# Routing two experts first, spreading small work over experts 1 and 2, and transposing act between two chunks of the down projection

## The chip, the cores and the metric

The kernel runs on one core of one Trainium2 chip. The metric is the device time of one execution in microseconds (us), as the median of several runs. Its engines are TensorE (PE, with its weight loads shown apart as PEld), VectorE (DVE), ScalarE (ACT), GpSimd (POOL, which here issues the indirect DMAs and some others) and SyncE (SP, which issues the weight loads).

## The reference, cut to what matters

The model is one layer: a sparse attention and a state-space branch are mixed, and then a mixture of 32 experts works on 512 tokens of width 1024. Only the experts are touched by the change.

```python
logits = (hf @ w_router + b_router)              # 512 tokens, 32 experts
top_val, top_idx = lax.top_k(logits, 4)          # four experts for each token
gates = softmax(top_val)
# for each expert, in blocks of 128 tokens:
gu = xb @ w_gu[e] + b_gu[e]                      # 1024 -> 2048
g, u = minimum(gu[:, :1024], 7), clip(gu[:, 1024:], -7, 7)
act = (u + 1.0) * (g * sigmoid(1.702 * g))
out = act @ w_dn[e] + b_dn[e]                    # 1024 -> 1024
x = x + g_f * sum over a token's experts of gate * out
```

## The kernel before

After the two branches, the kernel computes the router's logits, marks each token's four experts and ranks the tokens of each expert (`rankm`). Then it walks through the 32 experts, one block of 128 tokens each. A loop behind it (`tc.For_i`) takes experts with over 128 tokens; how often it turns is worked out as `nbt` from the counts `cnt`, through `more` and `cum`.

**Weights.** Each expert has twelve chunks of 1 MB (128 x 2048), eight for `w_gu` and four for `w_dn`. SP loads them in order into ten buffers. `msplit` makes two fp32r parts of each: ACT writes the high part (L1318), DVE the low part (L1319). PE multiplies three times per tile: high by high, high by low and low by high (L1468 to L1470), so that a chunk is 12 matmuls. Four split chunks stand ready; `refill` splits the next one when PE has used one up. The split tiles come from two pools in turn, `stm` (whi, wlo) and `M` (mhi, mlo).

**One expert.** An expert is two halves (f = 0, 1). Each half has a `group` for the gate columns (two chunks, with a bias matmul), a group for the up columns, four transposes of the next expert's tokens `xg` (L1270), and a group of the down projection of the expert before (`prev`). Behind that down group stand four transposes of this expert's `act`; ACT and DVE copy them as `ah` and `al`, which the next expert's down groups read. `gated` and `upped` (L1281, L1285, L1286) make `act` from the groups' sums, and L1533 scales the down result into `y`. From expert 1 on PE, DVE and ACT follow the order of the program text (`tc.manual_schedule`). POOL and SP do not: a planner orders their instructions. Expert 0 and all before it are ordered by the planner on every engine, except what `keep_in_program_order` pins.

**Routing.** For each expert a `one_hot` (128 x 512, L1004, DVE) is made, PE multiplies it with `aux` ("picks", into the PSUM tile `mi`), and a few small DVE operations turn the sums into `gi` (the rows to gather), `si` (the rows to add to) and `gate`. Expert 0 is routed alone, experts 1 to 3 together (`route(groups[0])`), and then four experts at a time in `routed`: its steps are queued and taken one by one by `hot_step`, which is called six times in an expert, behind each of its six groups. With four experts there are five steps that build a one-hot and pick the one before, and a sixth, `end`, that makes `gi`.

```python
groups = {0: [1, 2, 3]}
groups.update({e: list(range(e + 3, min(e + 7, NE))) for e in range(1, NE - 3, 4)})
```

The gates themselves are worked out late (`shares`, `gates_of`), behind expert 0's first gate group. The one-hots of pool `M` have two buffers.

**Gather and put.** `gather(e)` (POOL, L1376) brings the 128 token rows of expert e, 512 KB, from DRAM into `xg`, which has two buffers. In the text, expert e asks for the rows of expert e + 2 at its end, and expert e + 1 transposes them, the first half behind its first up group. `put` (POOL, L1289) adds `y` to the rows of the output in DRAM. Both use the same DMA queue.

```python
if f and e + 2 < NE:
    xg = gather(e + 2)
```

**Other work at the start.** `shared_biases` brings the down biases into a `y` tile, clears its last rows (L1396), and splits them; `shared_down(t)` (L1417, L1418) adds gates times biases to the output for each of four blocks of tokens. All four stand behind expert 0's second half, and the chain from `more` to `nbt` (L1452 to L1460) behind them.

Of the kernel before, what the change touches and what calls it, by code (L numbers as in the profile page):

```python
# [11 lines left out]
F32 = mybir.dt.float32  # L12
F32R = mybir.dt.float32r
BF = mybir.dt.bfloat16
I32 = mybir.dt.int32
# [7 lines left out]
P = 128  # L23
# [4 lines left out]
NE = 32  # L28
# [105 lines left out]
def program(tc, A, dbg=None, upto=99):  # L134
# [5 lines left out]
    with ctx:  # L140
# [66 lines left out]
        with ExitStack() as c1:  # L207
# [241 lines left out]
            for t in range(NT):  # L449
                T.transpose(p[:, t * P:(t + 1) * P], kin[:, t, :], ident)  # L450
            S.activation(kiT, p, AF.Identity, bias=gain[:, 3:4], scale=gain[:, 2:3])
            wi8 = con.tile([P, NT, 8], F32, name="wi8")
            V.tensor_scalar(wi8, s88[:, :, 64:72], 8 ** -0.5, None, op0=OP.mult)
            say("kiT", kiT, [P, L])

# [134 lines left out]
                                 scale=qk_gain[:, which:which + 1])  # L590


            cw = con.tile([P, 60], F32, name="cw")
            V.tensor_scalar(cw, convc, 0.5, None, op0=OP.mult)
            xdt = big("C", [P, NT, D])
            yD = quarters()
# [627 lines left out]
        def block_parts(M, mp, nbuf):  # L1224
# [61 lines left out]
                V.scalar_tensor_tensor(act, act, SILU7, u, op0=OP.min, op1=OP.mult)  # L1286

            def put(y, si, out=out):
                G.indirect_dma_start(out=out, out_offset=bass.IndirectOffsetOnAxis(ap=si, axis=0), in_=y,  # L1289
                                     in_offset=None, compute_op=OP.add)  # L1290

            def all_picked(p, i, hot, aux_of):
# [11 lines left out]
        with ExitStack() as c2:  # L1304
# [22 lines left out]
            def refill(pin=False):  # L1327
                if ahead:
                    parted.append(msplit(ahead.pop(0), pin))
                mload()  # L1330
# [24 lines left out]
                        T.matmul(p, x[1][:, kk, :], hi[:, ws], start=False, stop=(kk == KD - 1))  # L1355
                return p

            groups = {0: [1, 2, 3]}
            groups.update({e: list(range(e + 3, min(e + 7, NE))) for e in range(1, NE - 3, 4)})
            info = {}  # L1360

            def route(es):
# [27 lines left out]
            def shared_biases():  # L1390

                b = mt([P, KD, P], F32R, name="ah").rearrange("p k c -> p (k c)")
                raw = sized("y")
                for r in range(0, 96, 32):
                    G.dma_start(raw[r:r + 32, :], A["b_dn"])
                V.memset(raw[96:P, :], 0.0)  # L1396
                S.activation(b, raw, AF.Copy)
                V.tensor_tensor(b[32:64, :], raw[32:64, :], b[32:64, :].bitcast(F32), op=OP.subtract)
                gg = mt([P, 2, NT, P], F32R, name="al")
                gc, gT = gg[:, 0].rearrange("p t (a e) -> p t a e", e=NE), gg[:, 1]  # L1400
                V.memset(gc[:, :, 3, :].bitcast(F32), 0.0)
                for a in range(2):
                    V.tensor_copy(gc[:, :, a, :], gates)
                V.tensor_tensor(gc[:, :, 2, :], gates, gc[:, :, 0, :].bitcast(F32), op=OP.subtract)
                p = mp.tile([P, NT, P], F32, name="tr", tag="tr", bufs=2)
                for t in range(NT):
                    T.transpose(p[:, t, :], gg[:, 0, t, :].bitcast(F32), ident)
                S.activation(gT, p, AF.Copy)
                return gT, b
# [24 lines left out]
            for f in range(2):  # L1434
                fs = slice(f * 512, (f + 1) * 512)
                u = mt([P, 512], name="u", bufs=1)
                gated(act[:, fs], three(xT, bias["b_gu"], 0, f * 512, "gu", 3))
                if f == 0:
                    shares()
                    gates_of([0])  # L1440
                    gates_of(groups[0])
                upped(u, three(xT, bias["b_gu"], 0, FE + f * 512, "gu", 3), act[:, fs])
                if f == 0:
                    shared = shared_biases()
                    xT_next = transposed(xg, "x")
                    xg = gather(2)
                else:
                    for t in range(NT):
                        shared_down(t, *shared)
                aT = transposed(act, "a", b=f, into=aT, scale=1.0 / ALPHA)  # L1450
            few = mt([P, NE], name="few", bufs=1)
            tc.keep_in_program_order(V.tensor_scalar(more, cnt, 128.5, None, op0=OP.is_gt))  # L1452
            for lim in (256.5, 384.5):
                V.tensor_scalar(few, cnt, lim, None, op0=OP.is_gt)
                V.tensor_tensor(more, more, few, op=OP.add)
            V.tensor_copy(cum, more)
            for d in (1, 2, 4, 8, 16):
                V.tensor_copy(few, cum)
                V.tensor_tensor(cum[:, d:], few[:, d:], few[:, 0:NE - d], op=OP.add)
            V.tensor_copy(nbt, cum[:, NE - 1:NE])  # L1460

# [5 lines left out]
                    T.matmul(p, x[0][:, kk, :], lo[:, ws], start=False, stop=False)  # L1469
                    T.matmul(p, x[1][:, kk, :], hi[:, ws], start=False, stop=(kk == KD - 1))  # L1470

            def group(x, e, c0, take):
                if c0 is None:
                    p = mp.tile([P, 512], F32, name="dn", tag="dn", bufs=2)
                else:
# [4 lines left out]
                for i in range(2):  # L1480
                    chunk(p, x, i, c0 is None)
                    if i:
                        take(p)
                    refill()

            routing = []

            def hot_step():

                if routing:  # L1490
                    routing.pop(0)()

            def routed(es):
                p = mp.tile([P, 512], F32, name="mi", tag="mi", bufs=1)[:, 0:6 * len(es)].rearrange("p (e c) -> p e c", c=6)
                hots = {}

                def step(i):
                    if i:
                        all_picked(p, i - 1, hots.pop(i - 1), lambda t: aux[:, t, es[i - 1], :])
                    if i < len(es):  # L1500
                        hots[i] = one_hot(M, es[i])

                def end():
                    gi, si, gate = all_of(p, len(es))
                    for i, e in enumerate(es):
                        info[e] = gi[:, i:i + 1], si[:, i:i + 1], gate[:, i:i + 1]

                return [lambda i=i: step(i) for i in range(len(es) + 1)] + [end]

            with tc.manual_schedule(engines={mybir.EngineType.PE, mybir.EngineType.DVE, mybir.EngineType.Activation}):  # L1510
                for e in range(1, NE + 1):
                    prev, xT, aT = aT, xT_next, None
                    if e < NE:
                        act = sized("act")
                        xT_next = None
                    y = sized("y")
                    if e in groups:
                        routing += routed(groups[e])
                    if e == NE:
                        halves_ = M.tile([P, 2], I32, name="halves")  # L1520
                        for f in range(2):
                            V.tensor_scalar(halves_[:, f:f + 1], info[e - 1][1], 2.0, float(f), op0=OP.mult, op1=OP.add)
                    for f in range(2):
                        fs = slice(f * 512, (f + 1) * 512)
                        if e < NE:
# [4 lines left out]
                            if e + 1 < NE:  # L1530
                                xT_next = transposed(xg, "x", b=f, into=xT_next)
                            hot_step()
                        group(prev, e - 1, None, lambda p: V.scalar_tensor_tensor(  # L1533
                            y[:, fs], p, info[e - 1][2], gf[:, fs], op0=OP.mult, op1=OP.mult))
                        if e < NE:
                            aT = transposed(act, "a", b=f, into=aT, scale=1.0 / ALPHA)
                            hot_step()
                        else:
                            put(y[:, fs], halves_[:, f:f + 1], out.rearrange("r (h c) -> (r h) c", h=2))
                        if f and e + 2 < NE:  # L1540
                            xg = gather(e + 2)
                    if e < NE:
                        put(y, info[e - 1][1])


        with ExitStack() as c3:
# [108 lines left out]
```

## Time and profile before

| | |
|---|---|
| median of three runs | 1827.83 us (1823.12 to 1829.53) |
| the profiled execution's own time | 1832.19 us |
| its span, first to last instruction | 1830.4 us |
| PE busy | 1761.2 us, 96% of the span |
| DVE busy | 1541.3 us, 84% |
| ACT busy | 1074.2 us, 59% |
| weight loads and other hardware-queue DMA | 469.70 MB |
| mean granted TensorE clock | 0.973 |

Busy is the time in which an engine worked on an instruction; DMA issues, waits and branches don't count. A busy PE is not one at its peak, because the ends of its matmuls are modelled. The clock is the share of full speed that PE was granted. Idle time of an engine that isn't the bottleneck costs nothing.

### The profile page before, as it was taken

To read this page: it belongs to the slowest core of one execution; us is meant where nothing else is said; L and a number is where in the kernel's file an instruction comes from. 1 tells how busy PE (TensorE), PEld (TensorE's weight loads), DVE (VectorE), ACT (ScalarE), POOL (GpSimd) and SP (SyncE) were. 2 spreads that over 40 slices of the span, in tenths; PEclk is the share of its full clock that TensorE was granted. 3 is DMA by queue.
4 is the path that set the end of the run, shared out by engine and by line. 5 is a ranking of instruction groups with operands and counts; after the bars stand their busy time and mean duration, and the time that the engine had idled before them with its cause. 6 is when DMAs were issued, how large, how long until landed. Compare 5 with 4: busy or idle time off the path is not lost. (4 is left out here: it accounts for less than half of the span.)

```text
span 1830.4 us, 22578 instructions
## 1 busy us (share of the span) xinstructions
PE 1761.2 (96%) x8540; PEld 1396.5 (76%) x8540; DVE 1541.3 (84%) x1877; ACT 1074.2 (59%) x1059; POOL 195.3 (11%) x114
## 2 busy tenths in 40 slices
PE   6999999999999679999999999999999999999997
PEld 3866877776678567888888888888888888888885
DVE  6486678865676779999999999999999999999995
ACT  3443333444323356776777777777777777777773
POOL 0000000000000111111111211111111111111101
PEclk9988999998799889999999999999999999999998
DMA  8242334432475489999999999999999999999991
GB/s 318 80 143 75 115 141 167 152 129 79 179 264 210 172 275 335 397 376 370 379 381 367 381 377 379 370 377 378 368 375 382 367 384 388 341 399 379 372 361 40
DMA packets 86455, 527.24 MB, mean 288 GB/s; under 512 B 10912, under 2 KB 11072, under 8 KB 32072
## 3 DMA queue, kind: packets, MB, share of 16 engines
q1 hardware_dynamic: 70552, 469.70, 66.5%
q0 software_dynamic: 15552, 55.97, 11.1%
q8 instruction: 68, 1.11, 0.2%
q14 instruction: 43, 0.35, 0.1%
q10 hardware_dynamic: 240, 0.10, 0.0%
HBM read 497.91 MB, written 30.45 MB: 289 GB/s over the span
## 5 line engine op out<-in xcount | busy, mean ns | idle before, releaser
L1319 DVE TENSOR_TENSOR wlo<-raw,whi 128x2048 fp32r<-128x2048 f32 x154 | 352.2, 2288 | 31.8 <-ACT whi L1318 31.8
L1319 DVE TENSOR_TENSOR mlo<-raw,mhi 128x2048 fp32r<-128x2048 f32 (+1 forms) x160 | 352.5, 2207 | 24.6 <-ACT mhi L1318 22.1
L1318 ACT ACTIVATE whi<-raw 128x2048 fp32r<-128x2048 f32 x154 | 295.4, 1918 | 115.3 <-PE gu L1470 66.8
L1318 ACT ACTIVATE mhi<-raw 128x2048 fp32r<-128x2048 f32 (+1 forms) x160 | 296.0, 1854 | 108.5 <-PE gu L1470 61.8
L1468 PE MATMUL gu<-whi,xh 128*128 128x512 f32 x496 | 196.4, 396 | 0.0
L1470 PE MATMUL gu<-whi,xl 128*128 128x512 f32 x496 | 196.4, 396 | 0.0
L1469 PE MATMUL gu<-wlo,xh 128*128 128x512 f32 x496 | 196.2, 396 | 0.0
L1470 PE MATMUL gu<-mhi,xl 128*128 128x512 f32 x496 | 193.6, 390 | 0.0
L1469 PE MATMUL gu<-mlo,xh 128*128 128x512 f32 x496 | 193.3, 390 | 0.0
L1468 PE MATMUL gu<-mhi,xh 128*128 128x512 f32 x496 | 193.3, 390 | 0.0
L1289 POOL DMA_INDIRECT out_dram<-y,si x31 | 104.3, 3364 | 465.5 <-DVE y L1533 465.5
L393 PE MATMUL mm<-B,whi 128*128 128x512 f32 x352 | 141.0, 400 | 0.0
L392 PE MATMUL mm<-bA,whi 128*128 128x512 f32 x320 | 131.3, 411 | 2.0 <-DVE brow L661 1.0
L394 PE MATMUL mm<-bA,wlo 128*128 128x512 f32 x320 | 128.4, 402 | 0.8 <-DVE wlo L185 0.8
L1376 POOL DMA_INDIRECT xg<-h2d,gi x32 | 62.2, 1945 | 543.5 <-PE tr L1270 500.3
L184 ACT ACTIVATE whi<-raw 128x2048 fp32r<-128x2048 f32 x34 | 65.0, 1914 | 85.9 <-PE mm L393 72.3
L1469 PEld LDWEIGHTS gu<-wlo,xh 128*128 128x128 f32 x496 | 93.3, 188 | 22.5
L1470 PEld LDWEIGHTS gu<-whi,xl 128*128 128x128 f32 x496 | 93.2, 188 | 22.5
L1468 PEld LDWEIGHTS gu<-whi,xh 128*128 128x128 f32 x496 | 93.5, 188 | 20.9 <-ACT xh L1271 0.2
L1469 PEld LDWEIGHTS gu<-mlo,xh 128*128 128x128 f32 x496 | 93.1, 188 | 20.2
L1470 PEld LDWEIGHTS gu<-mhi,xl 128*128 128x128 f32 x496 | 93.1, 188 | 19.7
L1468 PEld LDWEIGHTS gu<-mhi,xh 128*128 128x128 f32 x496 | 93.3, 188 | 18.6
(471 smaller groups left out, 3703.7 us busy)
## 6 DMA issues: line engine op xcount, KB each, us to landing
raw<-in_w_gu_dram SPq DMA_DIRECT2D x204, 1024.0 KB
raw<-in_w_dn_dram SPq DMA_DIRECT2D x104, 1024.0 KB
B<-in_w_gu_dram SPq DMA_DIRECT2D x52, 1024.0 KB
B<-in_w_dn_dram SPq DMA_DIRECT2D x24, 1024.0 KB
raw<-in_w_in_dram SPq DMA_DIRECT2D x23, 1024.0 KB
rawp<-in_w_ada_dram POOLq DMA_DIRECT2D x30, 512.0 KB, 4.1
bE<-in_w_ada_dram SPq DMA_DIRECT2D x4, 1024.0 KB
bC<-in_x_dram SPq DMA_DIRECT2D x8, 512.0 KB
```

Of the source, the lines that this page charges most:

```text
L184: S.activation(hi[:, 0:n], raw[:, 0:n], AF.Copy)
L392: T.matmul(p, wh, xT[0][:, k, :], start=(k == 0), stop=False)
L393: T.matmul(p, wh, xT[1][:, k, :], start=False, stop=False)
L394: T.matmul(p, wl, xT[0][:, k, :], start=False, stop=(k == nk - 1))
L1289: G.indirect_dma_start(out=out, out_offset=bass.IndirectOffsetOnAxis(ap=si, axis=0), in_=y, in_offset=None, compute_op=OP.add)
L1318: S.activation(hi[:, cs], raw[:, cs], AF.Copy)
L1319: i = V.tensor_tensor(lo[:, cs], raw[:, cs], hi[:, cs].bitcast(F32), op=OP.subtract)
L1376: G.indirect_dma_start(out=xg, out_offset=None, in_=h2d, in_offset=bass.IndirectOffsetOnAxis(ap=info[e][0], axis=0))
L1468: T.matmul(p, x[0][:, kk, :], hi[:, ws], start=(start and kk == 0), stop=False)
L1469: T.matmul(p, x[0][:, kk, :], lo[:, ws], start=False, stop=False)
L1470: T.matmul(p, x[1][:, kk, :], hi[:, ws], start=False, stop=(kk == KD - 1))
```

## The change

Eight edits stand together. `wi8` and `cw` move from the pool that lives to the end (`con`) to the one of the first part (`W`). `put` returns its instruction. The first routed set is experts 1 and 2; experts 3 to 5 are routed within expert 1, and from expert 4 on the sets of four begin at e + 2 in place of e + 3. The clearing of the bias rows is pinned to its place in the text. Two of the four `shared_down` move into the first two `hot_step` of expert 1, and the `nbt` chain, cut into ten steps, into those of experts 2 and 3; `y` is taken behind them. In `routed` a pick follows its one-hot by two steps, and `end` shares the step of the last pick. The transposes of `act` move between the two chunks of the down group (`mid`). The puts of the last two down results go out in halves, and the very last one is tied to the second half of the result before and not to the first half of its own.

```diff
-            wi8 = con.tile([P, NT, 8], F32, name="wi8")
+            wi8 = W.tile([P, NT, 8], F32, name="wi8")
...
-            cw = con.tile([P, 60], F32, name="cw")
+            cw = W.tile([P, 60], F32, name="cw")
...
-                G.indirect_dma_start(out=out, out_offset=bass.IndirectOffsetOnAxis(ap=si, axis=0), in_=y,
+                return G.indirect_dma_start(out=out, out_offset=bass.IndirectOffsetOnAxis(ap=si, axis=0), in_=y,
...
-            groups = {0: [1, 2, 3]}
-            groups.update({e: list(range(e + 3, min(e + 7, NE))) for e in range(1, NE - 3, 4)})
+            groups = {0: [1, 2], 1: [3, 4, 5]}
+            groups.update({e: list(range(e + 2, min(e + 6, NE))) for e in range(4, NE - 2, 4)})
...
-                V.memset(raw[96:P, :], 0.0)
+                tc.keep_in_program_order(V.memset(raw[96:P, :], 0.0))
...
-                    for t in range(NT):
+                    for t in range(2):
                         shared_down(t, *shared)
...
-            tc.keep_in_program_order(V.tensor_scalar(more, cnt, 128.5, None, op0=OP.is_gt))
...
+            def blocks_step(i):
+
+                if i == 0:
+                    V.tensor_scalar(more, cnt, 128.5, None, op0=OP.is_gt)
+                elif i < 3:
+                    V.tensor_scalar(few, cnt, 128.0 * i + 128.5, None, op0=OP.is_gt)
+                    V.tensor_tensor(more, more, few, op=OP.add)
+                elif i == 3:
+                    V.tensor_copy(cum, more)
+                elif i < 9:
+                    d = 1 << (i - 4)
+                    V.tensor_copy(few, cum)
+                    V.tensor_tensor(cum[:, d:], few[:, d:], few[:, 0:NE - d], op=OP.add)
+                else:
+                    V.tensor_copy(nbt, cum[:, NE - 1:NE])
...
-            def group(x, e, c0, take):
+            def group(x, e, c0, take, mid=None):
...
                     refill()
-
-            routing = []
+                    if mid and not i:
+                        mid()
+
+            routing, extra, added = [], [], []
...
-                if routing:
-                    routing.pop(0)()
+                for todo in (routing, extra):
+                    if todo:
+                        todo.pop(0)()
...
-                    if i:
-                        all_picked(p, i - 1, hots.pop(i - 1), lambda t: aux[:, t, es[i - 1], :])
+                    if i > 1:
+                        all_picked(p, i - 2, hots.pop(i - 2), lambda t: aux[:, t, es[i - 2], :])
                     if i < len(es):
                         hots[i] = one_hot(M, es[i])
+                    elif i > len(es):
+                        end()
...
-                return [lambda i=i: step(i) for i in range(len(es) + 1)] + [end]
-
+                return [lambda i=i: step(i) for i in range(len(es) + 2)]
+
+            box = [aT]
...
-                    y = sized("y")
+                    y = None
                     if e in groups:
                         routing += routed(groups[e])
-                    if e == NE:
-                        halves_ = M.tile([P, 2], I32, name="halves")
+                    if e == 1:
+                        extra += [lambda t=t: shared_down(t, *shared) for t in (2, 3)]
+                    if e == 2:
+                        extra += [lambda i=i: blocks_step(i) for i in range(10)]
+                    split_put = e >= NE - 1
+                    if split_put:
+                        halves_ = mt([P, 2], I32, name="halves")
...
+                        if f == 0:
+                            y = sized("y")
+                        if e < NE:
+                            def mid():
+                                box[0] = transposed(act, "a", b=f, into=box[0], scale=1.0 / ALPHA)
                         group(prev, e - 1, None, lambda p: V.scalar_tensor_tensor(
-                            y[:, fs], p, info[e - 1][2], gf[:, fs], op0=OP.mult, op1=OP.mult))
-                        if e < NE:
-                            aT = transposed(act, "a", b=f, into=aT, scale=1.0 / ALPHA)
-                            hot_step()
-                        else:
-                            put(y[:, fs], halves_[:, f:f + 1], out.rearrange("r (h c) -> (r h) c", h=2))
+                            y[:, fs], p, info[e - 1][2], gf[:, fs], op0=OP.mult, op1=OP.mult), mid if e < NE else None)
+                        hot_step()
+                        if split_put:
+                            added.append(put(y[:, fs], halves_[:, f:f + 1], out.rearrange("r (h c) -> (r h) c", h=2)).ins)
                         if f and e + 2 < NE:
                             xg = gather(e + 2)
-                    if e < NE:
+                    if not split_put:
                         put(y, info[e - 1][1])
+
+
+                tc.declare_no_dep(added[3], added[2], reason="disjoint halves of the rows")
+                tc.add_manual_dep(added[3], added[1].name, mybir.DependencyInfo(
+                    mybir.DependencyClass.Sync, mybir.DependencyReason.DATA), reason="rows of the expert before")
```

## Rows read from the trace of the kernel before

**Rows 1.** Windows (us from the start): length, busy time (instructions) of each engine, clock, DMA.
```profile
663.47:694.23 30.76, 21.65 (x96) 17.21 (x95) 23.49 (x38) 12.93 (x12) 9.42 (x7) 0.83 0.90 261
...
1055.69:1073.70 18.01, 18.01 (x86) 14.66 (x84) 16.71 (x12) 12.98 (x10) 0.00 (x0) 1.00 1.02 398
...
1127.92:1147.02 19.10, 18.91 (x99) 14.99 (x97) 18.73 (x15) 12.95 (x10) 0.00 (x0) 1.00 0.97 376
```

**Rows 2.** Waits from 740 to 1790 us: us in total, times, longest.
```profile
ACT whi L1318 <- PE gu L1470: 78.2, 87, 1.2
...
PE mi L1294 <- DVE hot L1004: 1.3, 6, 0.2
```

**Rows 3.** Timeline of 655 to 680 us, DVE, POOL and PE.
```profile
659.84 0.69 DVE L1004 TENSOR_TENSOR hot<-cst,ranks 128x512 bf16<-128x512 f32 x1
...
663.63 3.00 POOL L1376 DMA_INDIRECT xg<-h2d,gi  x1 [33.09 <-DVE gate L1257]
...
672.33 1.97 PE L1270 MATMUL tr<-cst,xg 128*128 128x128 f32 x8 [8.57 <-DMA xg<-h2d,gi]
```

**Rows 4.** Windows behind two idle stretches of PE, columns as in rows 1.
```profile
672.30:678.00 5.70, 5.67 (x21) 4.66 (x22) 3.29 (x6) 1.79 (x3) 1.77 (x2) 0.53 0.76 292
1810.90:1814.00 3.10, 3.10 (x9) 2.38 (x9) 0.23 (x1) 0.00 (x0) 0.00 (x0) 0.50 0.96 160
```

**Rows 5.** Timeline of the last 25 us, PE, POOL and DVE.
```profile
1809.90 0.51 PE L1470 MATMUL dn<-whi,al 128*128 128x512 f32 x1 [1.83 <-DVE al L1276]
...
1815.74 1.54 POOL L1289 DMA_INDIRECT out_dram<-y,halves  x1 [5.08 <-DMA out_dram<-y,si]
...
1819.71 0.75 DVE L1533 SCALAR_TENSOR_TENSOR y<-dn,gate,gf 128x512 f32<-128x512 f32 x1 [5.18 <-PE dn L1470]
...
1821.34 1.54 POOL L1289 DMA_INDIRECT out_dram<-y,halves  x1 [4.07 <-DVE y L1533]
```

**Rows 6.** Timeline of 623 to 637 us, DVE and POOL.
```profile
624.88 0.91 DVE L1396 MEMSET y<- 32x1024 f32 x1 [0.27 <-issue]
...
627.09 2.38 POOL L1376 DMA_INDIRECT xg<-h2d,gi  x1 [6.43 <-DVE gi L1246]
```

**Rows 7.** Groups of DVE's instructions, 663.47 to 694.23 us: busy, mean ns, idle before.
```profile
L1418 DVE TENSOR_TENSOR y<-dn,gf 128x512 f32<-128x512 f32 x8 | 5.3, 684 | 1.6 <-DMA out_dram<-y 1.4 <-PE dn L1417 0.2
...
L1459 DVE TENSOR_TENSOR cum<-few 128x31 f32<-128x31 f32 (+3 forms) x4 | 0.7, 179 | 0.0
```

**Rows 8.** Timeline of one half of an expert without routing, DVE and PE.
```profile
1765.28 0.69 DVE L1286 SCALAR_TENSOR_TENSOR act<-act,u 128x512 f32<-128x512 f32 x1
...
1766.24 0.39 PE L1468 MATMUL dn<-mhi,ah 128*128 128x512 f32 x1
```

**Rows 9.** Timeline around the end of expert 5, which routes, PE, DVE and POOL.
```profile
861.93 0.60 PE L1270 MATMUL tr<-cst,act 128*128 128x128 f32 x4
...
863.58 0.74 DVE L1533 SCALAR_TENSOR_TENSOR y<-dn,gate,gf 128x512 f32<-128x512 f32 x1
...
864.61 3.34 POOL L1289 DMA_INDIRECT out_dram<-y,si  x1 [33.75 <-DVE y L1533]
...
867.45 0.17 DVE L1246 CAST gi<-q 128x4 int32<-128x4 f32 x1
...
868.41 3.07 POOL L1376 DMA_INDIRECT xg<-h2d,gi  x1 [0.46 <-PE gu L1470]
...
873.90 0.60 PE L1270 MATMUL tr<-cst,xg 128*128 128x128 f32 x4
```

**Rows 10.** Gathers, us from issue to landing: one right behind a put; all 32.
```profile
xg<-h2d,gi POOLq DMA_INDIRECT x1, 10.8
...
DMA to landing us min/median/max: 4.2/9.5/13.9
```

**Rows 11.** Costliest groups of the page: busy, mean ns, idle before.
```profile
L1468 PE MATMUL gu<-whi,xh 128*128 128x512 f32 x496 | 196.4, 396 | 0.0
...
L1468 PE MATMUL gu<-mhi,xh 128*128 128x512 f32 x496 | 193.3, 390 | 0.0
```

More of the change, by code (lines that the diff above doesn't have):

```diff
@@ L1451, in program @@
             few = mt([P, NE], name="few", bufs=1)
-            tc.keep_in_program_order(V.tensor_scalar(more, cnt, 128.5, None, op0=OP.is_gt))
[L1453 to L1460, printed above, removed]
+            def blocks_step(i):
[12 more added lines that the diff above has]
+                    V.tensor_copy(nbt, cum[:, NE - 1:NE])
             def chunk(p, x, i, start):
@@ L1506, in end @@
                         info[e] = gi[:, i:i + 1], si[:, i:i + 1], gate[:, i:i + 1]
-                return [lambda i=i: step(i) for i in range(len(es) + 1)] + [end]
+                return [lambda i=i: step(i) for i in range(len(es) + 2)]
+            box = [aT]
             with tc.manual_schedule(engines={mybir.EngineType.PE, mybir.EngineType.DVE, mybir.EngineType.Activation}):
                 for e in range(1, NE + 1):
-                    prev, xT, aT = aT, xT_next, None
+                    prev, xT, box = box[0], xT_next, [None]
                     if e < NE:
```

## The prediction

> **What bounds the kernel now.** I read the windows first, then the waits, then the timeline wherever PE stands idle, and last the DMA issues. In a plain half of an expert PE is busy for all of its 18.01 us, and DVE for 16.71 us; with routing the half takes 19.10 us [rows 1]. In the waits of the expert loop ACT waits for PE to free a split tile, 78.2 us in one row alone, while PE's only waits are those for a one-hot, 1.3 us in all; no engine waits for a weight load [rows 2]. So the loop runs at PE's pace, DVE has 1.3 us to spare in a half, and whatever stops PE there is paid in full.
>
> PE stops at two places. At the start it idles 8.57 us for the tokens of expert 1, whose gather begins only at 663.63 us [rows 3]: experts 1 to 3 are routed together, and expert 3's one-hot (659.84 us, same rows) needs a buffer that the picks of the gates still hold. Behind that gap the clock stands at 0.53 for 5.70 us, behind the short one near the end at 0.50 for 3.10 us [rows 4]; the lower level, 1.2 of 2.4 GHz, so about half of such a stretch is lost. At the end PE waits 1.83 us for `al`, and the last put begins late [rows 5].
>
> **The change part by part, the start.** The clearing of the bias rows, 0.91 us, now stands in the chain that makes expert 0's `gi`, for which the first gather waits [rows 6]. Pinned, it leaves that chain: 1.0 us (0 if the write of the token rows ended last, which no row shows; 1.2 with the idle 0.27 us ahead of it). Experts 1 and 2 alone fit the two one-hot buffers and need no gates, so the wait of 8.57 us goes, and with it 0.47 x 5.70 = 2.7 us of slow clock: 11.3 us by PE. What is late next is DVE. From 663.47 us to the end of expert 1's first `act` at 694.23 us it works 23.49 of 30.76 us [rows 1]. Two of the eight bias products of that stretch (0.68 us each) move behind it, 1.3 us, and so do the 13 small operations of the `nbt` chain at about 0.18 us, 2.4 us [rows 7]; the pinned clearing and the missing one-hot roughly cancel. DVE thus needs 19.8 us, 11.0 us less than the stretch took. I take 10 us in all, since a wait for the bias results' DMA (1.4 us in the same rows) will hardly shrink; 5 us if a new wait takes half, 12.5 us at most. In expert 1 the two products weigh 1.3 us each against DVE's spare 1.3 us in a half, and the chain's steps in experts 2 and 3 stay below 0.4 us each: hidden, and at worst 2 us if expert 1's two one-hots have used the spare time.
>
> **Transposes of act between the chunks.** They need `act`, which ends at 1765.28 + 0.69 = 1765.97 us; the matmul in whose place they come begins at 1766.24 us [rows 8]. The cover is 0.27 us, so I take 0. It is thin: DVE makes `act` in program order behind a split, and each 0.1 us by which it is late costs 62 x 0.1 = 6.2 us over the halves. That is the bound upward; a gain has no place in these halves, for the same four transposes run either way. Only the last expert gains, below.
>
> **Picks two steps behind.** Half a set's 1.09 us (19.10 less 18.01 us) I take for waits that go, as the rest is the picks themselves: 0.5 us x 6 sets = 3 us. But the one-hot behind the first gate group, 0.69 us, now delays `act` against the thin cover: 0.2 us x 6 back. I take -1.7 us, between -6.5 (the whole 1.09 us) and +2.5 us (0.4 us late in each).
>
> **The sets of four, one expert later.** This is the large term. In expert 4 the set is 6 to 9, its `gi` is made in the sixth and last `hot_step`, and the very next gather is that of expert 6; the same in experts 8, 12, 16, 20 and 24. Before, the set began at e + 3, and its first gather had a whole expert more. The times are those of expert 5 before, which routes in the same steps. Its down group ends at 861.93 us, `gi` at 867.45 + 0.17 = 867.62 us, and the transposes behind the next up group, which will read these very tokens, begin at 873.90 us [rows 9]. The put stands between: POOL holds it from 864.61 for 3.34 us, and the gather begins at 868.41 us. With the transposes of `act` ahead, DVE writes `y` some 0.6 us later (a copy of the size of the 0.69 us in rows 8), so put and gather move to 865.2 and 869.0 us. A gather right behind a put took 10.8 to 13.9 us to land in six cases [rows 10], 12.5 us in their mean. The tokens are there at 881.5 us: PE waits 7.6 us, with the down group of 24 matmuls queued behind the transposes. The wait resembles the 8.57 us one, so 2.5 us of slow clock follow (2.7 there, 1.5 behind the short one). 6 x (7.6 + 2.5) = 60.6 us. Landings of 10.8 and 13.9 us give 5.9 and 9.0 us, or 49 and 70 us in all. The set in expert 28 has two experts, ends in the fourth step, two groups earlier, and is hidden; that of expert 1 ends in the fifth, some 6 us earlier, and its gather lands about 2 us before its time by the median of 9.5 us, so 0, or 3 us where it queues behind the bias results, which now pass POOL beside it.
>
> That the matmuls behind the transposes can't pass them is the program order that the kernel sets. The Trainium skill (TensorE: Matmul & The Clock Gate, Step-by-step: what each phase is for) says so for the engine too: only weight loads are pulled ahead, matmuls keep their order. No row here shows a ready matmul behind a waiting one; if it could pass, the wait would shrink by the down group.
>
> **The end.** `al` comes early enough: 1.83 us and half of 3.10 us of slow clock go. The last `y` ends at 1820.46 us and its put begins 0.88 us later [rows 5], against 0.29 us in rows 9; tied to an earlier put, it saves 0.6 us, and the halves of the put before (1.54 us each for 3.34 us) cost nothing. Without the new tie the old chain of puts would eat most of it. Less 0.3 us for `act` at the last, shorter group: 3.7 us; 1.4 to 4.5 us.
>
> **Storage.** 368 bytes a partition move, which shifts other tiles. The two pools' matmuls differ by 396 and 390 ns [rows 11]; if the shift changed one kind into the other, 1,488 of them would give 9 us either way. Nothing says that address is the reason: 0.
>
> **Sum.** -10 - 1.7 - 3.7 + 60.6 = +45.2 us. The profiled execution took 1832.19 us, 1.8 us beyond its span, and would take 1877.4; it lies 4.4 us above the median and outside the three runs. The sum is of differences, so I add it to the median: 1873.0 us.
>
> **The rivals.** (1) POOL gathers before it puts. The text has that order, and the planner decides; for it to gather first it must foresee `gi` before `y`, while `y` is ready 3.3 us sooner, and in the six cases before the put went first. Then the gather begins at 868.4 us, lands 9.5 us later at 877.9 us, and PE waits 4.0 us and loses 2 us of clock: 36 - 15.4 = +20.6, 1848.4 us. (2) The other side: the gather is hidden, and only the gains stay, 1827.8 - 15.4 = 1812.4 us. For that it must land within 873.9 - 868.4 = 5.5 us. One of 32 landed in 4.2 us, the median is 9.5 us [rows 10]. It decides where the wait with its clock falls below 15.4 / 6 = 2.6 us, a landing of about 6.5 us. A page gives it a reason: the Trainium skill (DMA: Bandwidth & Descriptors, Anatomy of one DMA — SWDGE (gpsimd) path) fits such a DMA by 2 us plus its bytes at 436 GB/s, an estimate of 3.2 us for 512 KB, by which the time would be that of this rival. The rows don't bear it out. (3) The start doesn't get faster, because the planner sets the transposes of expert 1's tokens ahead of their landing or leaves `gi` behind the gates, and the waits come all the same: +55 us, 1883 us. The one-hots speak against it: with two there is no buffer to wait for.
>
> **Chances and range.** Put first, 0.58; gather first, 0.22; hidden, 0.10; no gain at the start, 0.06; the rest, a late `act` in every half or a change of the matmuls' pace on top, 0.04. The likeliest case's own range, from the landings and the bounds of the start, is 1860 to 1888 us. With the gather-first case, whose wait falls to some 2.5 us if all land in 8 us, 1840 to 1886 us should hold 8 in 10. A measurement of this kernel tells some 0.3% (5.5 us) from no change. Faster than that, 0.11; within it, 0.04; slower, 0.85.
>
> **What would show it.** Right: six waits of PE at L1270 for xg, some 145 us apart, in experts 5, 9, 13, 17, 21 and 25, each with a clock of one half behind it; no wait for the second gather near 664 us; no wait for `al` in the last down group; the last two puts one behind the other. Wrong: no such waits (the gathers begin earlier, or land in 6 us), PE waiting for `act` in every half, or a first `act` of expert 1 that comes no sooner than before.

## The result and the profile after

| | before | after |
|---|---|---|
| median of four runs each | 1825.47 us (1821.61 to 1829.53) | 1891.28 us (1888.95 to 1893.57) |
| ratio, 95% interval | | 1.036 (1.0331 to 1.039) |
| the profiled execution's time, span | 1832.19, 1830.4 us | 1888.95, 1887.1 us |
| mean granted clock | 0.973 | 0.961 |

Slower by 65.8 us, where the prediction had 45.2 us (1873.0; range 1840 to 1886). One execution of `before_filled`, a kernel of the experiments, ran in a slower state (1942.28 us, mean clock 0.841) and is left out of its figures. The two profiled executions differ by less, 56.7 us of span: the one of before lies 6.7 us above its median here, the one of after 2.3 us below, and 56.7 + 6.7 + 2.3 is the 65.8 us. Four marks in the timelines (starts of the bias matmuls at L1348 and L1486, L1479 before) say where the 56.7 us lie:

| stretch | before, us | after, us | difference | predicted |
|---|---|---|---|---|
| start to expert 0's second gate group | 655.74 | 658.41 | +2.7 | -1.0 |
| to expert 2's first group | 61.15 | 61.33 | +0.2 | -9.0 |
| to expert 30's first group | 1016.50 | 1073.64 | +57.1 | +58.9 |
| to the end | 97.02 | 93.76 | -3.3 | -3.7 |

PE's waits of after from 640 us on (us in total, times, longest), which answer to [rows 2, 3, 5]:

```profile
PE tr L1270 <- DMA xg<-h2d,gi: 45.5, 6, 9.8
PE dn L1475 <- DVE y L1418: 6.6, 1, 6.6
PE dn L1417 <- DVE y L1418: 2.3, 1, 2.3
PE tr L1270 <- DVE act L1286: 0.9, 4, 0.3
```

The six foretold waits for the tokens are there, 7.6 us in the mean (5.8 to 9.8 us singly). The 8.57 us wait and that for `al` are gone. New is a wait of PE's down group for `y` of L1418: a bias product. The transposes of `act` wait four times, 0.9 us in all.

The first of the six in the timelines of DVE, POOL and PE:

```profile
833.87 0.17 DVE L1246 CAST gi<-q 128x4 int32<-128x4 f32 x1
...
831.62 3.35 POOL L1289 DMA_INDIRECT out_dram<-y,si  x1 [33.41 <-DVE y L1556]
835.27 2.73 POOL L1376 DMA_INDIRECT xg<-h2d,gi  x1 [0.30 <-PE gu L1477]
838.30 2.22 POOL L1376 DMA_INDIRECT xg<-h2d,gi  x1 [0.30 <-issue]
...
849.50 1.09 PE L1270 MATMUL tr<-cst,xg 128*128 128x128 f32 x4 [8.89 <-DMA xg<-h2d,gi]
850.24 0.78 PE L1475 MATMUL dn<-whi,ah 128*128 128x512 f32 x1
```

The landing of that gather, from the DMA issues, and a window behind the wait (columns as in rows 1):

```profile
xg<-h2d,gi POOLq DMA_INDIRECT x1, 14.1
```

```profile
849.50:853.00 3.50, 3.50 (x11) 2.92 (x12) 0.69 (x1) 0.60 (x1) 0.00 (x0) 0.50 1.01 425
```

The put goes first, the gather follows at 835.27 us and lands 14.1 us later, at 849.36 us; PE, ready at 840.61 us, begins at 849.50 us, at a clock of 0.50. The down matmuls queued behind the transposes read `ah` and `al` of the expert before and start only then, at 850.24 us: matmuls kept their order. The Trainium skill (TensorE: Matmul & The Clock Gate, Step-by-step: what each phase is for) has it so, and the trace agrees.

Expert 1 holds the surprise. DVE, then the first down matmul on PE:

```profile
683.98 1.29 DVE L1418 TENSOR_TENSOR y<-dn,gf 128x512 f32<-128x512 f32 x2 [0.21 <-DMA out_dram<-y]
685.18 2.28 DVE L1319 TENSOR_TENSOR mlo<-raw,mhi 128x2048 fp32r<-128x2048 f32 x1
687.38 0.68 DVE L1285 TENSOR_SCALAR u<-gu 128x512 f32<-128x512 f32 x1
688.10 0.69 DVE L1286 SCALAR_TENSOR_TENSOR act<-act,u 128x512 f32<-128x512 f32 x1
688.71 2.28 DVE L1319 TENSOR_TENSOR mlo<-raw,mhi 128x2048 fp32r<-128x2048 f32 x1
690.91 0.68 DVE L1273 TENSOR_TENSOR xl<-tr,xh 128x512 fp32r<-128x512 f32 x1
691.51 0.68 DVE L1004 TENSOR_TENSOR hot<-cst,ranks 128x512 bf16<-128x512 f32 x1
692.11 1.28 DVE L1418 TENSOR_TENSOR y<-dn,gf 128x512 f32<-128x512 f32 x2
...
692.94 0.77 PE L1475 MATMUL dn<-whi,ah 128*128 128x512 f32 x1 [6.56 <-DVE y L1418]
```

The last product's two sums stand in the two `dn` buffers until DVE, in program order behind two splits, `act`, `xl` and a one-hot, reads them at 692.11 us. The down group needs one of these buffers and PE idles 6.56 us. Ahead of this the gain is there: expert 1's first `act` (the row of 688.10 us) ends 30.4 us behind the start of expert 0's second gate group (658.41 us), where before it ended 38.5 us behind it (694.23 us [rows 1], 655.74 us). The 8.1 us are lost again behind that `act`: from its end to expert 2's first group it is 31.0 us for 22.7 us before.

First gather (answers to [rows 6]), then the last puts and the last `y` ([rows 5]):

```profile
630.46 1.67 POOL L1376 DMA_INDIRECT xg<-h2d,gi  x1 [6.66 <-DMA h2d<-r]
...
1875.58 1.54 POOL L1289 DMA_INDIRECT out_dram<-y,halves  x1 [3.96 <-DMA out_dram<-y,halves]
1877.80 1.56 POOL L1289 DMA_INDIRECT out_dram<-y,halves  x1 [0.68 <-DVE y L1556]
...
1876.78 0.75 DVE L1556 SCALAR_TENSOR_TENSOR y<-dn,gate,gf 128x512 f32<-128x512 f32 x1 [4.86 <-PE dn L1477]
```

With the clearing out of the way the gather waits for the write of the token rows. The last put begins 0.27 us behind the last `y` (1877.53 us), for 0.88 us before.

### The profile page after: what moved, and what is told of

Read it like the earlier page. It is cut to its first block, busy times and chain, and to the rows that moved or that the text cites. A ratio compares the mean times of both kernels' runs of the same rounds, so it can differ in the third digit from the quotient of the medians.

```text
span 1887.1 us, 22583 instructions
## 1 busy us (share of the span) xinstructions
PE 1778.9 (94%) x8534; PEld 1403.2 (74%) x8536; DVE 1543.9 (82%) x1886; ACT 1074.7 (57%) x1059; POOL 199.4 (11%) x115
## 4 chain that ended last, share of the span: by engine, by line
PE 84%; DMA 6%; DVE 6%; issue 3%; ACT 1%; POOL 0%; SPq 0%; POOLq 0%; DVEq 0%; ACTq 0%
PE gu L1477 11%; PE gu L1476 11%; PE gu L1475 11%; PE dn L1475 6%; PE dn L1477 6%; PE dn L1476 6%; DMA xg<-h2d,gi 4%; PE mm L392 4%; PE mm L393 4%; PE mm L394 4%; PE tr L1270 3%; PE gu L1486 2%; PE ac L849 1%; PE at L821 1%; PE mm L384 1%
## 5 line engine op out<-in xcount | busy, mean ns | idle before, releaser
L1289 POOL DMA_INDIRECT out_dram<-y,si x30 | 99.7, 3323 | 592.3 <-DVE y L1556 592.0
L392 PE MATMUL mm<-bA,whi 128*128 128x512 f32 x320 | 132.1, 413 | 2.0 <-DVE brow L661 1.0
L394 PE MATMUL mm<-bA,wlo 128*128 128x512 f32 x320 | 128.8, 403 | 0.8 <-DVE wlo L185 0.8
L1475 PE MATMUL dn<-whi,ah 128*128 128x512 f32 x256 | 111.5, 436 | 6.6 <-DVE y L1418 6.6
```

The lines of the kernel that those rows point to most:

```text
L392: T.matmul(p, wh, xT[0][:, k, :], start=(k == 0), stop=False)
L394: T.matmul(p, wl, xT[0][:, k, :], start=False, stop=(k == nk - 1))
L1289: return G.indirect_dma_start(out=out, out_offset=bass.IndirectOffsetOnAxis(ap=si, axis=0), in_=y, in_offset=None, compute_op=OP.add)
L1475: T.matmul(p, x[0][:, kk, :], hi[:, ws], start=(start and kk == 0), stop=False)
```

## The experiments

Each ratio is to runs of the kernel before on the same chip, with its 95% interval; 0.001 is 1.8 us. Only `before_early_sets` and `gather_first` lie 2 to 3% from the kernel before; all others lie within 0.9% of it, and where two of their intervals overlap, the traces must help. A stretch is of the one profiled execution.

**The six sets.** `late_sets`, `before_early_sets`, `end_sooner` and `gather_first`, in this order:

```diff
-  range(e + 2, min(e + 6, NE)) ... for e in range(4, NE - 2, 4)   # after
+  range(e + 3, min(e + 7, NE)) ... for e in range(3, NE - 3, 4)
...
-  groups = {0: [1, 2, 3]}                                         # before
+  groups = {0: [1, 2, 3], 1: [4, 5]}
-  range(e + 3, min(e + 7, NE)) ... for e in range(1, NE - 3, 4)
+  range(e + 2, min(e + 6, NE)) ... for e in range(4, NE - 2, 4)
...
-  if i > 1: all_picked(p, i - 2, ...)                             # after
+  if i: all_picked(p, i - 1, ...)
-  elif i > len(es): end()      ...  range(len(es) + 2)
+  else: end()                  ...  range(len(es) + 1)
...
-  put(y, info[e - 1][1])                                          # after
+  tc.keep_in_program_order(put(y, info[e - 1][1]))
```

> The changed kernel with its sets of four begun at e + 3 again (6 to 9 in expert 3, and so on to 30 and 31 in expert 27), all other edits kept. Theory A (the six late gathers alone make the change slow, 9.3 us each with the clock behind them): the six waits of PE for xg vanish and the time falls by 56 us, from 1891 to about 1835 us, that is some 10 us above the kernel before, because the start gives its gain back. Rival B (the pace of the halves is worse: the transposes between the chunks, a late act, shifted storage): the waits vanish too, but at least a third of the 66 us stays, 1848 us or more.

> The kernel before with nothing but the sets moved: experts 4 and 5 routed within expert 1, and from expert 4 on sets of four begun at e + 2. Theory A: six waits of PE for xg of some 7 to 9 us with slow clock, 50 to 60 us slower than the kernel before, about 1881 us. Rival D (the waits need the put to be delayed by the moved transposes, or DVE to be later through the picks): waits below 4 us, 1850 us or less.

> The changed kernel, sets of four still begun at e + 2, but each pick one step behind its one-hot again and the making of gi in the step of the last pick: a set of four takes five steps, so gi is there behind the second up group, some 9 us sooner, and the gather is issued before that expert's last down group ends. Theory A (gi comes too late for the gather's landing): no wait of PE for xg in the six experts, 1891 less 56 to 60, about 1833 us. Rival F (what delays the landing is the queue full of puts and weight loads, whenever it is asked): waits of 4 us or more stay, 1860 us or more.

> The changed kernel with every put pinned behind the gather ahead of it in the text. gi is ready at the same time, so the gather starts only 1 us sooner (834.3 for 835.3 us in the first set). Theory A with the queue in it (a gather lands 7 us after its issue alone and 13 to 14 us behind a put): landing 7 to 10 us, waits of 0.7 to 4 us in place of 7.6, 1852 to 1872 us, about 1860. Rival G (only the late gi counts, the put ahead does not): the waits shrink by 1 us, 1884 us.

| kernel | median us | ratio | expert 2 to 30, us |
|---|---|---|---|
| `late_sets` | 1830.0 | 1.001 (0.999 to 1.0029) | 1016.96 |
| `before_early_sets` | 1882.12 | 1.0291 (1.0252 to 1.0331) | 1071.92 |
| `end_sooner` | 1827.92 | 1.0015 (0.9996 to 1.0034) | 1017.80 |
| `gather_first` | 1869.66 | 1.0221 (1.0176 to 1.0265) | 1060.92 |

Theory A's times hold in all four, and B, D and F fall: the sets alone make the kernel before slow, and without them the changed one is where the kernel before is. `end_sooner` shows that it is the lateness of `gi` and not the distance of two experts: one step sooner, and 0.8 us of wait for the tokens is left in all. `gather_first` separates the put's part. PE's wait for the tokens in it:

```profile
PE tr L1270 <- DMA xg<-h2d,gi: 32.0, 6, 6.5
```

Its first set in the timelines of POOL and PE:

```profile
826.74 2.95 POOL L1376 DMA_INDIRECT xg<-h2d,gi  x1 [36.59 <-PE gu L1476]
829.99 3.06 POOL L1289 DMA_INDIRECT out_dram<-y,si  x1 [0.30 <-issue]
...
837.86 1.09 PE L1270 MATMUL tr<-cst,xg 128*128 128x128 f32 x4 [5.33 <-DMA xg<-h2d,gi]
```

The waits shrink by 2.2 us each in the mean and the stretch by 12.7 us, so most of a wait, 5.3 of 7.6 us, is the late `gi`. Theory A's landing and waits (7 to 10 us, 0.7 to 4 us) missed: this gather lands 11.0 us after its issue (837.7 us), and the six 8.4 to 12.1 us. A put follows it 3.25 us later and may be why; that wasn't tried by itself. So 1869.66 us lies at the dear end of what A had, and far from G's 1884.

**The start.** From `late_sets`, the products back to expert 0 (`late_sets_shared0`), or three of the four (`late_sets_shared3`):

```diff
-  for t in range(2): shared_down(t, *shared)
+  for t in range(NT): shared_down(t, *shared)      # range(3) in shared3
-  if e == 1: extra += [... shared_down ... for t in (2, 3)]       # (3,) in shared3
```

> late_sets with all four bias products in expert 0, as in the kernel before. Theory A (the two products taken into expert 1 hold the two dn buffers until a late DVE frees them, and PE's first down group waits 6.6 us there, with slow clock behind): that wait vanishes, 8 us less than late_sets, about 1827 us. Rival C (DVE's work up to expert 1's first act is the bound, wherever the products stand): the wait moves to another place near expert 0's end and the time stays within 3 us of late_sets.

> late_sets with three bias products in expert 0 and only the last in the first step of expert 1. Theory A: the first down group finds a free buffer, since the product's DVE work ends some 8 us before that group begins: 8 us less than late_sets, about 1827 us, and like late_sets_shared0 or 1 us better. Rival C: within 3 us of late_sets.

And from the kernel before: the new routing order alone (`early_pair`), to it the two products in expert 1 (`pair_products`), or the pinned clearing and the chain of `nbt` in steps (`pair_blocks`):

```diff
-  groups = {0: [1, 2, 3]}
+  groups = {0: [1, 2], 1: [3, 4, 5]}
-  range(e + 3, min(e + 7, NE)) ... for e in range(1, NE - 3, 4)
+  range(e + 3, min(e + 7, NE)) ... for e in range(3, NE - 3, 4)
...
-  for t in range(NT): shared_down(t, *shared)
+  for t in range(2): shared_down(t, *shared)
+  if e == 1: extra += [lambda t=t: shared_down(t, *shared) for t in (2, 3)]
...
+  tc.keep_in_program_order(V.memset(raw[96:P, :], 0.0))
+  if e == 2: extra += [lambda i=i: blocks_step(i) for i in range(10)]
```

> The kernel before with only the routing order of the start changed: experts 1 and 2 ahead of the gates, 3 to 5 within expert 1, sets of four from expert 3 at e + 3; bias products, the nbt chain and all else as before. Theory A (the start's gain is real, and in the changed kernel the two bias products in expert 1 eat it): the 8.6 us wait for xg goes, DVE is late next, and 4 to 7 us are left of it, 1820 to 1823 us beside 1827. Rival H (the start gains nothing, since DVE's work ahead of expert 1's first act binds as much): the time of the kernel before within 2 us, with new waits of PE for DVE of 8 us or more in expert 1.

> early_pair with only the two last bias products moved into the first two steps of expert 1, as in the changed kernel. Theory A (these two products alone eat the start's gain): a wait of 5 to 7 us of PE's first down group for y, 5 to 8 us more than early_pair, a ratio of 0.999 to 1.000 to the kernel before. Rival L (the loss needs the clearing's pin, the late nbt chain or the moved transposes too): within 2 us of early_pair, 0.995 to 0.997.

> early_pair with only the clearing of the bias rows pinned and the nbt chain taken as steps of experts 2 and 3. By the prediction's sum these give 1.0 and 2.4 us: 2 to 3 us less than early_pair, a ratio of 0.994. Rival M (the planner, rid of the pinned start of that chain, orders expert 0's end otherwise and PE waits elsewhere, which is why kept loses 3.7 us to early_pair at the start): no gain or up to 4 us more than early_pair, 0.996 to 0.998.

| kernel | median us | ratio | expert 0's second gate group to expert 2, us |
|---|---|---|---|
| before, after, `late_sets` | | | 61.15, 61.33, 61.15 |
| `late_sets_shared0` | 1824.54 | 0.997 (0.9943 to 0.9996) | 56.12 |
| `late_sets_shared3` | 1828.34 | 1.0 (0.9981 to 1.0019) | 58.64 |
| `early_pair` | 1818.43 | 0.9956 (0.994 to 0.9972) | 54.94 |
| `pair_products` | 1827.12 | 1.0004 (0.9985 to 1.0024) | 58.49 |
| `pair_blocks` | 1823.33 | 0.9985 (0.9969 to 1.0001) | 57.99 |

The routing order alone takes 6.2 us from the stretch and 8 us from the time. Either of the other edits gives about half of the stretch back, 3.5 and 3.0 us, and both together, in `late_sets`, all of it. PE's waits from 640 us on, the largest of `early_pair`, of `pair_products`, and the two of `pair_blocks`:

```profile
PE mi L1294 <- DVE hot L1004: 6.3, 7, 5.0
```

```profile
PE dn L1468 <- DVE cum L1459: 7.7, 1, 7.7
```

```profile
PE mi L1294 <- DVE hot L1004: 7.3, 8, 5.4
PE dn L1417 <- DVE y L1418: 2.1, 1, 2.1
```

In `pair_products` the down group waits 7.7 us; the row names `cum`, the last thing that DVE did before, but in the timelines of DVE and PE it is again a late `y`:

```profile
683.55 0.68 DVE L1418 TENSOR_TENSOR y<-dn,gf 128x512 f32<-128x512 f32 x1
...
684.38 0.77 PE L1468 MATMUL dn<-whi,ah 128*128 128x512 f32 x1 [7.67 <-DVE cum L1459]
```

Theory A, not L or H. The other kernels bear it out: from the end of expert 1's first `act` to expert 2's first group, the five kernels with a product in the second step of expert 1 (`after`, `late_sets`, `end_sooner`, `gather_first`, `pair_products`) take 30.6 to 31.6 us, and the thirteen others 21.9 to 23.6 us. In `late_sets_shared0` the 6.3 us wait of the down group in `late_sets` falls to 1.4 us; a product's own wait for `y` stays, 2.1 us for 2.3. `late_sets_shared3` missed A's number, and rival C has it: within 3 us of `late_sets`, with the products' own matmuls waiting for `y`, 7.0 us in two waits.

`pair_blocks` lost 5.3 us by the ratios, in M's direction and beyond its 4 us, against the sum. What the planner did is to be seen in DVE's timelines, of `early_pair` and then of `pair_blocks`, whose second gate groups begin at 649.42 and 645.05 us:

```profile
618.34 0.91 DVE L1396 MEMSET y<- 32x1024 f32 x1 [0.27 <-DMA y<-in_b_dn_dram]
...
634.77 1.22 DVE L1398 TENSOR_TENSOR ah<-y,ah 32x1024 fp32r<-32x1024 f32 x1 [1.73 <-ACT ah L1397]
...
663.03 0.68 DVE L1418 TENSOR_TENSOR y<-dn,gf 128x512 f32<-128x512 f32 x1
```

```profile
646.70 0.91 DVE L1396 MEMSET y<- 32x1024 f32 x1 [0.27 <-issue]
...
651.17 1.21 DVE L1398 TENSOR_TENSOR ah<-y,ah 32x1024 fp32r<-32x1024 f32 x1
...
661.49 0.68 DVE L1418 TENSOR_TENSOR y<-dn,gf 128x512 f32<-128x512 f32 x1
```

Pinned, the clearing and the split of the biases that needs it (L1398) stand behind that mark, some 2.4 us of DVE with the 0.27 us, and the first product comes 16.4 us behind it, not 13.6. The clearing stands there in all nine kernels with the pin and in none without it. The pin without the chain was not run.

**Small terms.** The end and the moved transposes, with the moved storage (`mid_end`) and without it on `early_pair` (`pair_mid_end`), and the storage alone:

```diff
-  wi8 = con.tile ...   cw = con.tile ...
+  wi8 = W.tile ...     cw = W.tile ...             # all of storage_only
...
+  if mid and not i: mid()                          # mid_end, pair_mid_end
+  split_put = e >= NE - 1   ...   added.append(put(y[:, fs], halves_[:, f:f + 1], ...).ins)
```

> The kernel before with the storage of wi8 and cw moved, the transposes of act between the two chunks of the down group, and the last two puts in halves; routing, sets and bias products as before. Theory A: nothing in the halves, 3.7 us less at the end, about 1822 us beside 1826. Rival B (act is late in every half): 6 us more or worse, 1828 us and above, with a wait of PE for act at the transposes in most experts.

> The kernel before with only wi8 and cw moved to the first part's pool. Theory A: the move does nothing, within 2 us of 1826 us. Rival E (the shifted addresses, or what they do to the stretch of half clock at 446 to 476 us, cost the 3 to 4 us that the late sets kernel still has over the kernel before): 1829 to 1830 us, with a stretch of half clock of 34 us instead of 31.

> early_pair with the transposes of act between the two chunks and the last two puts in halves, storage and all else as before. If the start's gain (a ratio of 0.9956) and the end's 3.7 us are independent: 0.9935, about 1815 us beside 1827, no wait for al in the last down group, and better than kept. Rival B (late act in the halves eats the end): 0.9956 or above.

`mid_end` took 1827.66 us (0.9995, 0.997 to 1.0019), `pair_mid_end` 1821.02 us (0.9961, 0.9947 to 0.9975), `storage_only` 1832.27 us (1.0026, 1.0008 to 1.0044). By ratio the end's gain is not to be seen; in the profiles it is: from expert 30 to the end 93.65 us in `mid_end`, for 97.02 before, and the stretch between experts 2 and 30 is 1016.34 us, so the transposes cost nothing there. In `mid_end` the storage can hide it. In `pair_mid_end`, with the old storage, theory A's 0.9935 was missed and B's number met, though not by B's late `act`: the three stretches are 55.33, 1017.25 and 93.67 us. Its runs had mean clocks of 0.974 to 0.98 where those of `early_pair` had 0.976 to 0.983; what took the 3.4 us is not shown. Matmuls of the first part, 240 to 430 us, before and in `storage_only` (busy, mean ns):

```profile
L392 PE MATMUL mm<-bA,whi 128*128 128x512 f32 x177 | 71.9, 406 | 0.5 <-DVE brow L661 0.5
```

```profile
L392 PE MATMUL mm<-bA,whi 128*128 128x512 f32 x177 | 72.4, 409 | 0.5 <-DVE brow L661 0.5
```

Rival E, which the prediction had put at nothing, is right about the cost, though its stretch of half clock was shorter (23.9 us) in the profile and not longer. The same row has a mean of 409 or 410 ns in all eight kernels with the moved tiles and of 406 or 407 ns in the ten others, and from the start of one such matmul to the next it is 232 ns in the median in the eight and 227 ns in the ten. There are 1,152 of these matmuls (three lines, L392 to L394): by the longer means, 3 and 2 ns, some 2.7 us, and by the steps at most 5.8 us, an estimate beside the 4.7 us of the ratio. `kept` is `late_sets_shared0` with the old storage (and one tile for both `halves`):

> late_sets_shared0 with wi8 and cw in their old pool. Theory A with the storage's price in it (3 to 5 us by storage_only): 3 to 5 us under late_sets_shared0 by its ratio to the kernel before, 0.994 to 0.995, about 1817 us beside 1827, with the matmuls of 240 to 430 us at 406, 396 and 397 ns as in the kernel before. Rival I (storage_only was scatter): the ratio of late_sets_shared0, 0.997.

1817.71 us, 0.9948 (0.993 to 0.9965): 4 us better than `late_sets_shared0` by ratios whose intervals overlap, and the three matmuls back at 406, 396 and 397 ns. In its profile the stretch to expert 2 is worse, 60.65 us for 56.12: DVE has the same order of work in both, but the first two bias products took 7.0 and 8.8 us to land in `out`, for 5.2 and 5.8 us, and DVE, which needs their `y`, and PE behind it wait the longer. So one profile can be some 4 us off in this stretch where all four products stand in expert 0.

**The half clock ahead of the experts.** Runs of one kernel scatter by 10 us and more. In the profiles a stretch of half clock begins near 445 us, behind an idle time of PE, and lasts 30.7 us before, 34.1 us after and in `late_sets`, and didn't come at all in one execution, of `late_sets_shared3`, where PE had idled for the same 2.4 us. Windows of before and of that one:

```profile
455.00:465.00 10.00, 10.00 (x34) 6.89 (x34) 4.03 (x18) 1.43 (x3) 0.53 (x1) 0.50 0.16 52
```

```profile
451.00:461.00 10.00, 10.00 (x61) 6.37 (x59) 8.50 (x22) 5.72 (x12) 0.53 (x1) 1.00 0.22 80
```

So one product there was done five times over, to fill the idle time (0.7 us of it were left):

```diff
-  T.matmul(p[0:1, 0:256], ones[:, 0:1], acc, start=True, stop=True)
+  for _ in range(5 if j == 10 else 1):
+      T.matmul(p[0:1, 0:256], ones[:, 0:1], acc, start=True, stop=True)
```

> The kernel before, with one small product of the first part (a row of the modulation, at 442 us) done five times over in place of once, which gives the same result and fills some 2.4 us in which PE idles there. Theory J (PE's idle time at 442 to 445 us is what the half clock of 446 to 476 us follows, and that stretch is what scatters the runs): no half clock there, 13 to 15 us less, about 1812 us beside 1827, and a narrower scatter. Rival K (the half clock follows something else): the stretch stays, within 2 us of the kernel before.

> kept with the same product done five times. If the two gains are independent: kept less 13 to 15 us, about 1803 us, a ratio of 0.986 to 0.988 to the kernel before. By rival K: the time of kept.

> pair_mid_end with the small product at 442 us done five times. before_filled gave a ratio of 0.9957 and a half clock stretch behind that place of 6.8 us in place of 30.7; if independent, 0.989, about 1807 us. If the filling does nothing by itself (its stretch was as long as others in kept_filled): 0.9935.

1819.31 us (0.9957, 0.9941 to 0.9972), 1811.36 us (0.9913, 0.9889 to 0.9937) and 1814.85 us (0.9932, 0.991 to 0.9954). Each is 5 to 8 us better than without the filling, half of what J had: the stretch became 6.8 us in the first and third profile, but was 20.5 us in `kept_filled`, as in `kept`, and unfilled kernels had anything from 0 to 34.1 us. So the gain rests on the times, with mean clocks of 0.979 to 0.983 in `before_filled` and 0.973 to 0.98 in the kernel before beside it. The idle time has a part in it; it isn't all. The two last kernels beat both the one before and the one after.

## Why the prediction was right and wrong

**The sets: right.** 45.5 us of waits where the sum had 6 x 7.6 = 45.6; that close by luck, as the single waits are 5.8 to 9.8 us. With the clock behind them the six cost 56.3 us between the spans of after and `late_sets` (1887.1 and 1830.8 us), 10.8 us of it beside the waits, 1.8 each where I had 2.5. The put came first as said. The rival that the gather comes first was priced at a landing of 9.5 us; run as `gather_first` it landed after some 11.

**The end: right**, 3.3 us of 3.7. **The transposes: right.** Of the picks' 1.7 us nothing is to be seen: experts 2 to 30 take 0.5 us more in `late_sets` than before, with one more set (of two, in expert 27) among them.

**The start: wrong, and this is the step that failed.** "In expert 1 the two products weigh 1.3 us each against DVE's spare 1.3 us in a half ... hidden, and at worst 2 us." I counted DVE's time and not when it gets to it. A product holds both `dn` buffers from its matmuls until DVE, which keeps the order of the text, has done what stands ahead, and the next down group on PE needs those buffers. Up to expert 1's first `act` the sum held, 8.1 us of its 9 to 10; behind it 8.3 us were lost where it had none, or 2 us at worst. Tried alone the two products gave 3.5 us of the stretch back, 8.8 us by the ratios (1.0004 less 0.9956, give or take 4.6). A second step failed beside it, that "the pinned clearing and the missing one-hot roughly cancel": the pin took the split of the biases along, 2.4 us in place of 0.9 us. The 3.4 us for the clearing and the chain came out as a loss of 3.0 us in the stretch; its size stays open, since `kept`, with both, is no slower than `pair_mid_end`, with neither (0.9948, 0.9961). In place of -10 us stands about 0, and 1873 becomes 1883 us. The third rival had this outcome, no gain at the start, by another mechanism, at 0.06.

**The storage: wrong.** Put at 0, it costs 4.7 us by its ratio (1.5 to 8.0 us by the interval). The bound of 9 us "if the shift changed one kind into the other" looked at the experts' matmuls; the price fell due in the first part. With the 57.1 us between experts 2 and 30 for 58.9, and the end's 3.3 for 3.7, the sum becomes 1883 - 1.8 + 0.4 + 4.7 = 1886.3 us. The 5.0 us left to the median of after are no more than the interval of its ratio allows (5.4 us either way); the half clock near 445 us may be in them, which isn't shown, since a run without a profile has only its mean clock.

**The hidden gather** (rival 2) had a page of the Trainium skill for it. All 32 gathers of after, issue to landing:

```profile
DMA to landing us min/median/max: 4.5/10.1/15.6
```

The Trainium skill (DMA: Bandwidth & Descriptors, Anatomy of one DMA — SWDGE (gpsimd) path) gives 3.2 us by its fit, an estimate; the trace doesn't agree, 4.5 us at best and 10.1 in the median beside a stream of weights, and the measurement decides.

## What to carry to other kernels

When work is moved into a tightly ordered stretch, count not only whether an engine has the time, but which buffer the moved step holds until that engine gets to it, and who needs the buffer next. Before an instruction is pinned, look for what depends on it and will move with it. An index that a gather needs should be ready a landing ahead, and the landing taken from gathers that have a put beside them. Split the difference of two profiles at fixed marks before explaining a median: here four stretches told at once which terms of the sum had come true.

## What the runs showed of the hardware

The time of one kernel goes with its mean granted clock: of 25 runs of the kernel before, those at 0.979 to 0.98 took 1821.8 to 1824.7 us, those at 0.972 to 0.973 1830.2 to 1833.8 us. Moving two tiles, 368 bytes a partition, to another pool changed the mean of a matmul from 406 to 409 ns; that the shifted addresses are the reason is likely but not shown. A gather of 512 KB landed 11.0 to 15.0 us after its issue behind a put (six of after), 8.4 to 12.1 us when a put followed 1 to 3 us later (six of `gather_first`), and in 4.5 us at the soonest (after).
